# Residual additions of a feed-forward layer by accumulating DMA, and five blocks a layer with all chunks by seven products

## The chip, the cores and the metric

The kernel runs on one core of a Trainium2 chip. The metric is the device time of one execution in microseconds (us); lower is better. The five engines of the core are called PE (TensorE, the matrix engine, with PEld for its weight loads), DVE (VectorE), ACT (ScalarE), POOL (GpSimd) and SP (SyncE, which here only issues DMAs).

## What is computed

One decoder layer over 256 tokens of width 2048: a feed-forward layer, a mixer (attention with selected keys beside a recurrent branch), and a second feed-forward layer, each followed by a layer norm. The change concerns the two feed-forward layers, which are, cut to what matters:

```python
def swiglu(h, w_in, w_out):
    a, b = jnp.split(h @ w_in, 2, axis=-1)        # w_in 2048 x 11264
    return (jax.nn.silu(a) * b) @ w_out           # w_out 5632 x 2048

h = layer_norm(DN_ALPHA * h + 0.5 * swiglu(h, ffn1_w_in[l], ffn1_w_out[l]), ln1_g[l], ln1_b[l])
# ... mixer, layer norm ...
h = layer_norm(DN_ALPHA * h + 0.5 * swiglu(h, ffn2_w_in[l], ffn2_w_out[l]), ln3_g[l], ln3_b[l])
```

All values are float32.

## The kernel before

Every large product is made of three matmuls on two rounded halves: an operand is split into a high part (a rounding copy by ACT) and a low part (the difference, by DVE), and `three` (L597) sums high x high, high x low and low x high into PSUM. For weights this is done piece by piece on the fly: `Weights.load_to` (L153) issues the loads on SP, eight pieces ahead, and `split_to` (L181) makes `wh` on ACT (L209) and `wl` on DVE (L210), four pieces ahead of PE. There are five buffers for each of `wh` and `wl`.

A feed-forward layer goes through 22 blocks of 256 hidden columns (512 columns of `w_in`, a and b together). `blockF` (L623) makes one block's product with `w_in`. The 2048 input rows are four chunks. A **plain** chunk is two pieces of 1024 columns; each piece is 12 matmuls of 512 columns (two row tiles, two token halves, three matmuls). A **fast** chunk uses a seven-product scheme on 2 x 2 sub-blocks (token halves, row tiles against columns a and b): it needs sums of weights, made by DVE (`operand`, L174: the `ws` sum L182 of 1024 columns, the sums L186 and L189 of 512), and sums of the input, made once per layer by `left` (L509). It has four pieces, `p1q3`, `p2`, `q5p7`, `q4p6`, with 12, 6, 12 and 12 matmuls of 256 columns. Its weight tile of 1 MB (`rf`) has two buffers, the plain pieces of 512 KB (`raw`) four, the sums `ws` one. The partial sums of a block lie in two banks `mm` (`c`) and, for the fast chunks, in two banks `bp` (`e`).

The gate of a block (`gate`, L886) joins the partial sums on DVE (L894 to L899), takes silu on ACT and multiplies on DVE (L905). Some pieces later PE transposes the result (L911), and `g` is split like the weights (L724, L725).

The product with `w_out` runs in the same loop. Pieces of it, called fills (`"o"` in a plan), stand between the pieces of later blocks; a fill is 12 matmuls of 512 columns. After two or four fills one 256 x 512 part of the layer's output is complete for one segment of blocks (`SEGS`), and `y_add` (L732) adds half of it to the residual tile `Y` on DVE (L734), once for each token half. The last segment's part is made after the last block, by `out_product`, where `y_add` also takes the statistics of the layer norm.

`block_plan` (L68) writes the order of the pieces in a block and `layer_plans` (L94) those of the 22 blocks. Blocks 0 and 1 are plain; of the rest most have chunks 1 to 3 fast and chunk 0 plain, four fills, and blocks 2 to 5 two or three fast chunks and two fills. From block 9 on the plan of a block is

```
o o c0 p1q3.1 p2.1 q5p7.1 o q4p6.1 p1q3.2 p2.2 c2 q5p7.2 q4p6.2 p1q3.3 o p2.3 q5p7.3 q4p6.3
```

PE, SP and POOL execute in the order in which the program is written; the order on DVE and ACT is a scheduler's, by priority and its own estimate of time. Small tasks (gate, transposes, `left`) are put between the pieces by `Background.step`, one step per piece.

Of the kernel before, what the change touches and what calls it, by code (L numbers as in the profile page):

```python
# [12 lines left out]
OP = mybir.AluOpType  # L13
# [49 lines left out]
PIECE = 1024  # L63
FAST = (1, 2, 3)
FAST_A = (2, 3)


def block_plan(chunks, fills, lead=2, n=4):  # L68
# [6 lines left out]
    plan = [(rest.pop(), 0) for _ in range(min(lead, fills))] + [plain.pop(0)]  # L75
    slow = []
    while plain or rest:
        for which in (rest, plain) if lead == 2 else (plain, rest):
# [200 lines left out]
def tile_layer(ctx, tc, x_fm, x_tm, pos, f1a, f1o, wA, wki, wB, wG, lru, wab, wrb, wo, f2a, f2o,  # L279
# [19 lines left out]
    def T1(s="t"):  # L299
        return pool.tile([P, S], F32, name=name(s), tag="t", bufs=T_BUFS)  # L300

# [72 lines left out]
    W = Weights(nc, pool, pieces, bg.step)  # L374
    W.fast_pool = ctx.enter_context(tc.tile_pool(name="f1", bufs=1))


# [131 lines left out]
    def left(src, forms, k):  # L509


        s = U("sf")
        a = [v.rearrange("p (t c) -> p t c", t=2) for v in src]
        q = s.rearrange("p (f c) -> p f c", f=4)
        V.tensor_tensor(q[:, 0], a[0][:, 1], a[1][:, 1], op=OP.subtract)
        V.tensor_tensor(q[:, 2], a[0][:, 0], a[0][:, 1], op=OP.subtract)
        V.tensor_tensor(q[:, 1], q[:, 0], a[0][:, 0], op=OP.subtract)
        V.tensor_tensor(q[:, 3], a[1][:, 0], q[:, 1], op=OP.add)
        h, l = U("sh", F32R), U("sl", F32R)
        A.activation(h, s, AF.Copy)  # L520
        V.tensor_tensor(l, s, h, op=OP.subtract)
        forms[k] = h, l
# [100 lines left out]
    def blockF(x, forms, plan, fill):  # L623

        c = e = None

        seen = set()
        last = {f: i for i, (f, k) in enumerate(plan)}  # L630
        top = max(last["c"], last.get("p2", 0)), max(last["c"], last.get("q4p6", 0))
        k0 = next(k for f, k in plan if f == "c")
        skip = 0
        if getattr(x, "halves", None):
            c = [MM(), MM()]
            eager(x, c)
            skip = 4
        for i, (form, k) in enumerate(plan):
            if i < skip:
                continue  # L640
            if form == "o":
                fill()
                continue
            if form == "c":
                if not c:
                    c = [MM(), MM()]
                    half = [c[0][:, :S], c[0][:, S:], c[1][:, :S]]
                for k in range(k, k + 2):
                    w = W.unit(512)
                    for t in range(2):  # L650
                        tokens(c[t], x[k], t, w, k == k0, k % 2 == 1 and i == top[t])
                continue
            if not e:
                e = [BP(), BP()]
                p1, p6, p7, q5 = e[0][:, :S], e[0][:, S:], e[1][:, :S], e[1][:, S:]
            start = form not in seen
            seen.add(form)
            stop = i == last[form]
            fs = [forms[2 * k + r] for r in range(2)]

            def xop(r, i, t):
                v = x[4 * k + 2 * r + i]
                return v[:, 0, t * P:(t + 1) * P], v[:, 1, t * P:(t + 1) * P]

            def sop(r, i):
                return tuple(v[:, i * P:(i + 1) * P] for v in fs[r])

            def run(ps, op, start, stop):
                for r in range(2):
                    three(ps, *op(r), W.unit(S), start and r == 0, stop and r == 1)  # L670

            if form == "p1q3":
                run(p1, lambda r: xop(r, 0, 0), start, False)
                run(half[1], lambda r: sop(r, 3), False, False)
            elif form == "p2":
                run(half[0], lambda r: xop(r, 1, 0), False, i == top[0])
            elif form == "q5p7":
                run(q5, lambda r: sop(r, 0), start, False)
                run(p7, lambda r: sop(r, 2), False, stop)
            else:  # L680
                run(half[2], lambda r: xop(r, 1, 1), False, i == top[1])
                run(p6, lambda r: sop(r, 1), False, stop)
        return c, e
# [47 lines left out]

    def y_add(ps, nb, stat, t):  # L732
        y = Y[t][nb]
        V.scalar_tensor_tensor(y, ps[t], 0.5, y, op0=OP.mult, op1=OP.add)  # L734
        if stat:
            V.bn_stats(stats["st"][t][:, nb * 6:nb * 6 + 6], y)  # L736

# [108 lines left out]
    def out_product(x, ln, forms=None, pair=False):  # L846
# [3 lines left out]
        def done(nb, ps, t):  # L850
            y_add(ps, nb, ln, t)
            if ln and nb == 3:
                ln.chain(t)
# [17 lines left out]
        for nb in range(len(ready), 4):  # L871
            if ln and nb == 3:
                ps = blockA(x, lambda ps: end(ps, 0), LAG_LAST if ln.last else LAG_LN,
                            None if ln.last else ln)
                end(ps, 1)
            else:
# [3 lines left out]
                for t in range(2):  # L880
                    done(nb, ps, t)
        if ln and ln.last:
            ln.finish()

    def ffn(x, forms, ln):
        def gate(c, e, g, i, lag):  # L886

# [3 lines left out]
            if e:  # L891
# [5 lines left out]
                for t in range(2):  # L897
                    zt = z[:, t * 512:(t + 1) * 512]
                    V.tensor_tensor(zt, zt, c[t], op=OP.add)  # L899
                A.activation(a, a, AF.Silu)  # L900
# [20 lines left out]
        def fill():  # L921
# [19 lines left out]
        if not ln.last:  # L941
            bg.add("main", later(consts(), W.last.ins))
        out_product(g[-1], ln, pair=True)
# [358 lines left out]
    out_product(mg, ln, mg_forms)  # L1302
    mg = mg_forms = None


# [77 lines left out]
```

## Time and profile before

| | |
|---|---|
| time, median of 3 runs | 2396.58 us (2395.66 to 2397.06) |
| profiled execution, its own time | 2395.88 us |
| its span, first to last instruction | 2394.1 us |
| mean granted clock of PE | 0.998 of full speed |
| PE, DVE, ACT busy | 99%, 92%, 60% of the span |
| DMA | 480.23 MB, mean 201 GB/s |

A page of the profile gives busy time by engine and by group of instructions; a row of a group reads: line, engine, operation, output <- input, shapes, count, then busy us, mean ns of one, and the idle time of the engine just before them with what ended it. A window gives the busy time of each engine in a stretch. A timeline lists instructions with start and duration in us. Instructions of one engine overlap by their start-up, so the pace of an engine is read from the distance between starts.

### The profile page before, as it was taken

How to read it: one execution, taken by the hardware profiler on the slowest of the kernel's cores; microseconds unless marked ns; L12 is line 12 of the kernel's file. 1: busy time of each engine (PE TensorE's matmuls, PEld its weight loads, DVE VectorE, ACT ScalarE, POOL GpSimd, SP SyncE). 2: the span in 40 equal slices, each digit the busy share in tenths (PEclk: the TensorE clock that was granted, in tenths of full speed). 3: DMA queues.
4: the chain of work that ended last, by engine and by line, in shares of the span. 5: the costliest groups of instructions: out<-in, count | busy, mean ns of one | idle time of the engine just before them, and what ended most of it. 6: DMA issues, size and time to landing. Idle time of an engine off the chain costs nothing. (4 is left out here: it accounts for less than half of the span.)

```text
span 2394.1 us, 38065 instructions
## 1 busy us (share of the span) xinstructions
PE 2371.3 (99%) x14674; PEld 2104.5 (88%) x14674; DVE 2209.0 (92%) x3127; ACT 1444.5 (60%) x1934; POOL 54.2 (2%) x118
## 2 busy tenths in 40 slices
PE   9999999999999999999999999999999999999997
PEld 7888889888888888888999998888889888888986
DVE  7999999999999998789788888998999999999997
ACT  7555555555547554665588885545655555555652
POOL 0000000000000000001000001100000000000000
PEclk9999999999999999999999999999999999999999
DMA  8555455555566456547655568755654555556554
GB/s 301 187 206 191 183 211 212 199 197 194 183 186 220 176 185 182 187 142 267 201 183 187 186 192 300 245 194 177 217 204 186 211 198 184 183 201 224 211 191 139
DMA packets 113286, 480.23 MB, mean 201 GB/s; under 512 B 13232, under 2 KB 13232, under 8 KB 93776
## 3 DMA queue, kind: packets, MB, share of 16 engines
q1 hardware_dynamic: 105984, 454.60, 54.1%
q0 software_dynamic: 7120, 23.19, 2.9%
q8 instruction: 115, 1.88, 0.3%
q14 instruction: 67, 0.55, 0.1%
HBM read 467.26 MB, written 10.49 MB: 200 GB/s over the span
## 5 line engine op out<-in xcount | busy, mean ns | idle before, releaser
L209 ACT ACTIVATE wh<-raw 128x1024 fp32r<-128x1024 f32 (+2 forms) x564 | 583.4, 1045 | 390.3 <-PE mm L600 252.0
L210 DVE TENSOR_TENSOR wl<-raw,wh 128x1024 fp32r<-128x1024 f32 (+2 forms) x564 | 669.2, 1197 | 91.6 <-ACT wh L209 89.6
L209 ACT ACTIVATE wh<-rf 128x1024 fp32r<-128x1024 f32 (+1 forms) x453 | 410.6, 916 | 265.3 <-PE mm L600 182.1
L210 DVE TENSOR_TENSOR wl<-rf,wh 128x1024 fp32r<-128x1024 f32 (+1 forms) x453 | 468.5, 1040 | 8.5 <-ACT wh L209 4.8
L598 PE MATMUL mm<-wh,hs 128*128 128x512 f32 (+1 forms) x908 | 329.3, 363 | 0.3 <-DVE z L899 0.3
L600 PE MATMUL mm<-wh,hs 128*128 128x512 f32 (+1 forms) x908 | 323.6, 356 | 1.1 <-DVE hs L786 1.1
L599 PE MATMUL mm<-wl,hs 128*128 128x512 f32 (+1 forms) x908 | 323.2, 356 | 0.2 <-DVE wl L210 0.2
L598 PE MATMUL mm<-wh,g 128*128 128x512 f32 x704 | 280.4, 398 | 0.0
L600 PE MATMUL mm<-wh,g 128*128 128x512 f32 x704 | 278.1, 395 | 0.0
L599 PE MATMUL mm<-wl,g 128*128 128x512 f32 x704 | 277.9, 395 | 0.0
L209 ACT ACTIVATE wh<-ws 128x1024 fp32r<-128x1024 f32 x151 | 160.1, 1061 | 175.2 <-PE mm L600 69.2
L598 PE MATMUL bp<-wh,sh 128*128 128x256 f32 x906 | 254.0, 280 | 0.0
L599 PE MATMUL bp<-wl,sh 128*128 128x256 f32 x906 | 252.9, 279 | 0.7 <-DVE wl L210 0.7
L600 PE MATMUL bp<-wh,sl 128*128 128x256 f32 x906 | 253.2, 279 | 0.0
L210 DVE TENSOR_TENSOR wl<-ws,wh 128x1024 fp32r<-128x1024 f32 x151 | 183.8, 1217 | 18.9 <-ACT wh L209 18.8
L600 PEld LDWEIGHTS mm<-wh,hs 128*128 128x128 f32 x908 | 170.4, 188 | 30.0 <-DVE hs L786 2.5
L598 PEld LDWEIGHTS mm<-wh,hs 128*128 128x128 f32 x908 | 170.6, 188 | 29.2 <-issue 4.4
L599 PEld LDWEIGHTS mm<-wl,hs 128*128 128x128 f32 x908 | 170.7, 188 | 24.7 <-DVE wl L210 0.7
L182 DVE TENSOR_TENSOR ws<-rf 128x1024 f32<-128x1024 f32 x151 | 183.9, 1218 | 4.6 <-DMA rf<-wA 1.4
L1217 PE MATMUL mm<-hs,wh 128*128 128x256 f32 x640 | 179.9, 281 | 0.0
L1216 PE MATMUL mm<-hs,wh 128*128 128x256 f32 x640 | 179.9, 281 | 0.0
L1218 PE MATMUL mm<-hs,wl 128*128 128x256 f32 x640 | 179.9, 281 | 0.0
(293 smaller groups left out, 5093.9 us busy)
## 6 DMA issues: line engine op xcount, KB each, us to landing
rf<-f1a SPq DMA_DIRECT2D x58, 1024.0 KB, 4.9
rf<-f2a SPq DMA_DIRECT2D x58, 1024.0 KB, 5.0
raw<-f1o SPq DMA_DIRECT2D x88, 512.0 KB, 5.8
raw<-f2o SPq DMA_DIRECT2D x88, 512.0 KB, 6.1
raw<-wB SPq DMA_DIRECT2D x80, 512.0 KB, 4.3
raw<-f2a SPq DMA_DIRECT2D x60, 512.0 KB, 4.8
raw<-f1a SPq DMA_DIRECT2D x59, 512.0 KB, 5.5
raw<-wG SPq DMA_DIRECT2D x54, 512.0 KB, 4.3
```

What stands on the lines that cost most here:

```text
L182: v.tensor_tensor(t, b[:, 0:4:3], b[:, 1:2].to_broadcast([P, 2, 2, 256]), op=OP.add)
L209: nc.scalar.activation(hp, src, AF.Copy)
L210: self.last = nc.vector.tensor_tensor(lp, src, hp, op=OP.subtract)
L598: T.matmul(ps, xh, w[0], start=start, stop=False)
L599: T.matmul(ps, xh, w[1], start=False, stop=False)
L600: T.matmul(ps, xl, w[0], start=False, stop=stop)
L1216: T.matmul(ps[:, :S], w[0], x[:, 0], start=first, stop=False)
L1217: T.matmul(ps[:, :S], w[0], x[:, 1], start=False, stop=False)
L1218: T.matmul(ps[:, :S], w[1], x[:, 0], start=False, stop=last)
```

## The change

- The fills' additions to `Y` leave DVE. ACT copies each finished half, times 0.5, from PSUM to a tile `yd`, and a DMA issued by POOL adds it to `Y` in place.
- Blocks 9, 12, 15, 18 and 21 of each layer take all four chunks by seven products; `blockF` no longer needs a plain chunk to open the banks, and starts and stops of the partial sums are worked out per bank.
- The order within blocks changes: every block from 6 on leads with three fills, blocks 3 to 5 all have three fast chunks. A block with four fast chunks is

```
o o o p1q3.0 p2.0 q5p7.0 q4p6.0 p1q3.1 p2.1 q5p7.1 q4p6.1 o p1q3.2 p2.2 q5p7.2 q4p6.2 p1q3.3 p2.3 q5p7.3 q4p6.3
```

- The joining part of the gate is issued at high priority.
- `left` is also made for chunk 0 in feed-forward layers (two calls more a layer). Its result lies in a pool that shares its space with the small tiles `t`, which are not used at that time.

```diff
-FAST = (1, 2, 3)
+FAST = (0, 1, 2, 3)
+BANKS = {"c": (0, 1), "p1q3": (2, 0), "p2": (0,), "q5p7": (3,), "q4p6": (1, 2)}
...
+FOUR = (9, 12, 15, 18, 21)
+
 def layer_plans():
     three = (1, 2, 3)
-    return ([block_plan((), 0)] * 2 + [block_plan((1, 3), 2, 0), block_plan(three, 2)] * 2
-            + [block_plan(three, 4, 3)] * 3 + [block_plan(three, 4)] * 13)
+    plans = [block_plan((), 0)] * 2
+    plans += [block_plan((1, 3), 2, 0)] + [block_plan(three, 2, 2, late=False)] * 3
+    for n in range(6, NBK):
+        plans.append(block_plan(FAST if n in FOUR else three, 4, 3))
+    return plans
...
+    lane, first_home, shared = [None], {}, ExitStack()
+    def share(which):
+        shared.close()
+        p = shared.enter_context(tc.tile_pool(name=name(which), bufs=1))
+        lane[0] = p if which == "t" else None
+        first_home.clear()
+        if which == "s":
+            first_home.update({0: p, 1: p})
...
-        h, l = U("sh", F32R), U("sl", F32R)
+        if k in first_home:
+            h, l = (first_home[0].tile([P, 512], F32R, name=name("s0"), tag="s0", bufs=4) for _ in range(2))
+        else:
+            h, l = U("sh", F32R), U("sl", F32R)
...
                 for t in range(2):
-                    zt = z[:, t * 512:(t + 1) * 512]
-                    V.tensor_tensor(zt, zt, c[t], op=OP.add)
+                    w = 512 if plain or t == 0 else S
+                    zt = z[:, t * 512:t * 512 + w]
+                    V.tensor_tensor(zt, zt, c[t][:, :w], op=OP.add)
...
             if k0 + 2 == len(g[s]):
                 for t in range(2):
-                    y_add(open_ps, nb, False, t)
+                    u = W.fast_pool.tile([P, 512], F32, name=name("yd"), tag="yd", bufs=2)
+                    A.activation(u, open_ps[t], AF.Copy, scale=0.5)
+                    G.dma_start(Y[t][nb], u, accum_op=OP.add)
...
                 c, e = blockF(x, forms, PLANS[n], fill)
-                task = gate(c, e, g[s], 2 * (n - b0), LAG_T[n == NBK - 1])
-                next(task)
+                task = gate(c, e, g[s], 2 * (n - b0), LAG_T[n == NBK - 1], ("c", 0) in PLANS[n])
+                with tc.high_priority():
+                    next(task)
                 bg.add("gate", task)
```

More of the change, by code (lines that the diff above doesn't have):

```diff
@@ L74, in block_plan @@
     rest = ["o"] * fills
-    plan = [(rest.pop(), 0) for _ in range(min(lead, fills))] + [plain.pop(0)]
+    plan = [(rest.pop(), 0) for _ in range(min(lead, fills))] + plain[:1]
+    plain = plain[1:]
     slow = []
     while plain or rest:
-        for which in (rest, plain) if lead == 2 else (plain, rest):
+        for which in (plain, rest) if late else (rest, plain):
             if which:
@@ L627, in blockF @@
         c = e = None
[L629 to L632, printed above, removed]
+        first, last = {}, {}
+        for i, (f, k) in enumerate(plan):
+            for b in BANKS.get(f, ()):
+                first.setdefault(b, i)
+                last[b] = i
         skip = 0
@@ L643, in blockF @@
                 continue
+            if not c:
+                c = [MM(), MM()]
+            start, stop = ([f.get(b) == i for b in range(4)] for f in (first, last))
             if form == "c":
[L645 to L648, printed above, removed]
+                for j in (k, k + 1):
                     w = W.unit(512)
                     for t in range(2):
-                        tokens(c[t], x[k], t, w, k == k0, k % 2 == 1 and i == top[t])
+                        tokens(c[t], x[j], t, w, start[t] and j == k, stop[t] and j > k)
                 continue
@@ L1303, in tile_layer @@
     mg = mg_forms = None
+    share("s")
     ffn(ln.hs, ln.forms, OuterNorm(ln3_g, ln3_b))
```

55 lines of the change are left out of this document (27 added, 28 removed).

## The prediction

> **What bounds the kernel now.** I read the page's engine table first, then the windows of a stretch that is nothing but feed-forward blocks, then the timelines of PE and DVE inside one block, because a share of 99% says that PE is never empty but not how much room the engine behind it has.
>
> ```profile
> PE 2371.3 (99%) x14674; PEld 2104.5 (88%) x14674; DVE 2209.0 (92%) x3127; ACT 1444.5 (60%) x1934; POOL 54.2 (2%) x118
> ...
> 1950.00:2300.00 350.00, 350.00 (x2211) 312.94 (x2210) 339.56 (x406) 206.32 (x242) 1.61 (x3) 1.00 0.55 200
> ```
>
> The second row is the window from 1950 to 2300 us (length; busy PE, PEld, DVE, ACT, POOL; clock; DMA share). PE is busy in all 350.00 us at full clock, DVE in 339.56, or 97.0%; ACT has 41% free. So every matmul cycle taken from these blocks shortens the run, but only while DVE, which makes each weight piece, keeps up. The timelines (start, duration) give both paces:
>
> ```profile
> 2012.90 0.28 PE L598 MATMUL mm<-wh,hs 128*128 128x256 f32 x1
> 2037.87 0.28 PE L598 MATMUL bp<-wh,sh 128*128 128x256 f32 x1
> 2039.27 0.28 PE L598 MATMUL mm<-wh,hs 128*128 128x256 f32 x1
> 2040.78 0.28 PE L599 MATMUL bp<-wl,hs 128*128 128x256 f32 x1
> 2042.07 0.40 PE L598 MATMUL mm<-wh,g 128*128 128x512 f32 x1
> 2044.87 0.28 PE L598 MATMUL mm<-wh,hs 128*128 128x256 f32 x1
> ...
> 2036.65 1.22 DVE L210 TENSOR_TENSOR wl<-rf,wh 128x1024 fp32r<-128x1024 f32 x1
> 2037.79 1.22 DVE L210 TENSOR_TENSOR wl<-raw,wh 128x1024 fp32r<-128x1024 f32 x1
> 2038.93 0.68 DVE L186 TENSOR_TENSOR rf<-ws,rf 128x512 f32<-128x512 f32 x1
> 2039.53 0.68 DVE L210 TENSOR_TENSOR wl<-rf,wh 128x512 fp32r<-128x512 f32 x1
> 2040.13 0.68 DVE L189 TENSOR_TENSOR rf<-rf 128x512 f32<-128x512 f32 x1
> 2040.73 1.22 DVE L210 TENSOR_TENSOR wl<-ws,wh 128x1024 fp32r<-128x1024 f32 x1
> ...
> 2043.17 1.22 DVE L182 TENSOR_TENSOR ws<-rf 128x1024 f32<-128x1024 f32 x1
> 2044.30 1.22 DVE L210 TENSOR_TENSOR wl<-raw,wh 128x1024 fp32r<-128x1024 f32 x1
> ```
>
> Durations overlap, so I go by starts. The fill piece from 2042.07 to 2044.87 is 12 matmuls of 512 columns: 2.80 us, 233.3 ns each. The q5p7 piece from 2037.87 to 2039.27 is 12 matmuls of 256: 1.40 us, 116.7 ns each, exactly half. The rows at 2012.90 and 2044.87 are the same step of two neighbouring blocks: 31.97 us per block. Of that, six plain or fill pieces are 16.80 and three chunks of 42 half-width matmuls 14.70; the other 0.47 are the gate's transposes. DVE takes 1.14 us per 1024-wide operation (2036.65 to 2037.79) and 0.60 per 512-wide one (2038.93 to 2039.53).
>
> The DVE row at 2036.65 writes the low half of the last p1q3 piece of its block; it ends at 2037.87, and PE first uses it at 2040.78. So DVE is 2.9 us ahead there, and this is the smallest such distance I found in that stretch: PE does not wait for DVE, but DVE's whole reserve is about one p1q3 piece and a half.
>
> **The change, PE's part.** A plain chunk is 24 matmuls of 512, 24 x 233.3 = 5.60 us. By seven products it is 42 of 256, 42 x 116.7 = 4.90 us. 0.70 us are saved per chunk. Converted are chunk 0 in the five blocks named in FOUR, and also chunk 2 of block 4, whose plan goes from two fast chunks to three: six a layer, twelve in two layers, 12 x 0.70 = **8.4 us**. The built program agrees on the count: 216 more matmul rows, 12 x 18. Everything from the first layer norm to the second feed-forward layer keeps its instruction order on all engines, so I put no gain or loss there.
>
> On weight loads one rule speaks against splitting matmuls: "TensorE: Matmul & The Clock Gate" of the Trainium skill (Back-to-back issue gap) gives a sustained 131 ns at 512 columns and 81 at 128, so that halving the width saves less than half. An estimate by that page, midway at 256, is 98 ns, a chunk then costs 0.97 us more and the change 12 us. The rows here show 233.3 and 116.7, so the sum stays with the rows.
>
> **DVE's part.** Four things change. (a) The 80 residual additions of the fills, L734, leave DVE:
>
> ```profile
> L734 DVE SCALAR_TENSOR_TENSOR y<-mm,y 128x512 f32<-128x512 f32 x22 | 14.1, 682 | 0.0
> ```
>
> That is the same window, about 11 blocks: 14.1 / 11 = 1.28 us a block. (b) A converted chunk costs DVE the ws sum and three wl of 1024, 4 x 1.14, and one wl and two sums of 512, 3 x 0.60: 6.36 us, against two wl of a plain one, 2.28: +4.1. (c) Chunk 0 needs its left forms, two calls a layer, in blocks 0 and 1, where all is plain and DVE has two 1.14 us operations per 5.6 us of PE: free. (d) In a four-chunk block the second half of the second bank is not added, -0.3 (half of a 512-wide operation).
>
> Per block, DVE now needs 339.56 x 31.97 / 350 = 31.0 us of 31.97. After: a three-chunk block 31.0 - 1.3 = 29.7 against 31.97, 2.3 to spare; a four-chunk block 29.7 + 4.1 = 33.8 against 31.97 - 0.70 = 31.27, **2.5 short**. FOUR has every third block, so three blocks need 93.0 of PE's 95.2 us: DVE can follow on the mean at 97.7%, and the question is whether the reserve lasts through one four-chunk block.
>
> I followed one by its order. Let PE start its first fill at 0. Three fills end at 8.4, then p1q3, p2, q5p7 and the transposes, q4p6 ends at 13.77, chunk 1 at 18.67, the fourth fill at 21.47, chunk 2 at 26.37; in chunk 3 q5p7 is due at 28.47 and q4p6 at 29.87. There are five hi/lo pairs, so chunk 1's p1q3 can be split when the third fill leaves PE at 8.4. The ACT copy before it
>
> ```profile
> L209 ACT ACTIVATE wh<-rf 128x1024 fp32r<-128x1024 f32 x66 | 70.2, 1064 | 26.6 <-PE mm L600 21.5 <-PE bp L600 3.8
> ```
>
> is free to start some 0.2 us later and takes 1.06, so DVE begins at about 9.7. From there its order leaves it no pause: up to the end of chunk 3's q5p7 stand eleven operations of 1.14, eight of 0.60 and two g splits,
>
> ```profile
> L725 DVE TENSOR_TENSOR g<-bp,g 128x256 fp32r<-128x256 f32 x22 | 9.2, 416 | 0.0
> ```
>
> 9.2 / 22 = 0.42 each: 18.2 us in all. Ready at 27.9, due at 28.47: **0.6 us to spare.** q4p6 follows at 29.0, due 29.87; the next block's first fill at 30.2, due 31.27.
>
> Two other covers are as thin. The weight loads: chunk 2's 1 MB tile is loaded into the one that chunk 0's last split frees at about 9.3, and is wanted at 14.7, 5.4 us later:
>
> ```profile
> DMA to landing us min/median/max: 4.8/4.9/7.0
> ```
>
> (the rf loads of the window). The median fits by 0.5 us; a landing of 7.0 takes 1.6 and would use up the cover. And blocks 3 to 5, with two fills, run short of DVE already:
>
> ```profile
> 1765.43 1.21 DVE L210 TENSOR_TENSOR wl<-ws,wh 128x1024 fp32r<-128x1024 f32 x1
> ...
> 1767.92 0.28 PE L599 MATMUL bp<-wl,sh 128*128 128x256 f32 x1
> ```
>
> At the end of block 3 the piece is ready at 1766.64 for 1767.92: 1.3 us ahead. Without L734 it would be 2.6. Such a block is PE 31.97 - 5.60 = 26.37 and DVE 29.7 - 2.28 = 27.4, 1.1 short; today block 4 with two fast chunks lets DVE recover, after the change three short blocks follow each other: 2.6, 1.5, 0.4 ahead. Still no stall; without cover up to 1 us a layer.
>
> **ACT, Pool, DMA.** ACT gains per block two reads of PSUM, 0.6 us each by the nearest row,
>
> ```profile
> L1162 ACT ACTIVATE gt<-mm x10: 577/598/600, 936.9 to 1468.8; 128x512 f32<-128x512 f32 x10
> y<-ys POOLq DMA_DIRECT2D x8, 256.0 KB, 4.3
> 1470.24 4.34 POOL L1169 DMA_DIRECT2D gf<-gd  x8
> ...
> 1471.60 1.23 DVE L182 TENSOR_TENSOR ws<-rf 128x1024 f32<-128x1024 f32 x1
> 1472.74 1.22 DVE L210 TENSOR_TENSOR wl<-raw,wh 128x1024 fp32r<-128x1024 f32 x1
> ```
>
> and 1.06 us for each extra copy. They wait in ACT's queue for the fourth fill to end, at 21.47; behind them is the copy for chunk 3's p1q3, which could not start earlier anyway, because the same fill holds its buffer. 0.2 + 1.2 + 1.06 later, at 23.9, it is there; DVE, by the same count, comes to it at 23.8. That pause takes 0.1 of the 0.6. So I forecast no stall in the four-chunk blocks, with half a microsecond of cover in each. No accumulating DMA is in the trace; by the nearest row a 256 KB transfer issued by Pool lands after 4.3 us, its u tile is wanted again a block later and its Y tile four blocks later. Bounds: 4.3 to 31 us cost nothing, above that ACT would wait. Pool issues one in 0.54 us (eight in 4.34). Whether DVE is held meanwhile: during those eight its 1024-wide operations start 1.14 us apart (1471.60 to 1472.74), as elsewhere, so I take nothing; the other bound is 80 x 0.54 = 43 us of DVE. "SBUF — State Buffer" of the Trainium skill (the rule on the shared port pair) has a DVE operation with two SBUF inputs collide with Pool's reads, not its writes; the rows agree. On Pool's queue ln3's row loads now stand behind the accumulations; only the final normalisation, after the last matmul, wants them.
>
> Small gain: where the plan passes from three leading fills to two, PE waited once a layer for the gate to free its bank. All later blocks lead with three after the change.
>
> ```profile
> L598 PE MATMUL mm<-wh,hs 128*128 128x512 f32 x600 | 241.6, 403 | 0.3 <-DVE z L899 0.3
> ```
>
> 0.3 us, twice. I set it against small waits that thin covers invite.
>
> **Sum.** The profiled execution is 2395.88 us, its span 2394.1; the runs' median 2396.58 is 0.7 above it. Span 2394.1 - 8.4 = 2385.7, and **2388.2 us** against the median. About 0.2%, 4.8 us, is what a measurement of this kernel can tell from no change; faster by that means under 2391.8, slower over 2401.4.
>
> **Rivals.**
> A, the covers fall short by a little. Every number above is a start-to-start time without the spread of 16 queues or of semaphores, and DVE takes its work in a fixed order. A stall of 0.4 to 1.3 us in each of ten four-chunk blocks gives 4 to 13 us back: 2392 to 2401, no difference that can be told. For it: three covers under 0.7 us. Against it: PE had not one stall behind DVE in 350 us at 97.0%. 0.19.
> B, slower: DVE does not bring its reserve back in the three-chunk blocks, because the gate's additions now go first and its pauses stay (the window leaves it 10.4 us in 11 blocks, most of it a wait for ACT).
>
> ```profile
> L210 DVE TENSOR_TENSOR wl<-ws,wh 128x1024 fp32r<-128x1024 f32 x33 | 40.2, 1219 | 6.6 <-ACT wh L209 6.6
> ```
>
> Then each four-chunk block stalls by its whole 2.5 us, or more: 25 - 8.4, 2413. It decides from 1.3 us of stall per four-chunk block. Against it: that wait is for a copy which itself waits for PE to free a buffer, so it goes when DVE is behind. 0.12.
> C, half-width matmuls become bound by their weight loads, 188 ns each instead of 116.7:
>
> ```profile
> L598 PEld LDWEIGHTS mm<-wh,hs 128*128 128x128 f32 x908 | 170.6, 188 | 29.2 <-issue 4.4
> ```
>
> 42 x 188 is 2.3 us above a plain chunk, 12 of them 28 us: 2424. The 1.40 us of q5p7 speak against it. 0.01.
> D, the change does not do what it says: an accumulation lands so late that the last block's sums hold the final additions, which read the same Y tiles. Landing in 4.3 us against some 17 us to the first of them (six fill pieces) speaks against it. All of the 8.4 us would be gone: 2396. 0.02.
> The forecast has 0.66.
>
> **Numbers.** Faster 0.66 + a little of A's edge = 0.67; same 0.20; slower 0.13. The range: from 2386.5 (the two waits, 0.6, and a spread of 1) to 2397, which takes in the forecast and most of A.
>
> **What would show it.** By layer, 144 fewer matmuls of 512 columns and 252 more of 256. Right: PE busy in all of 1950 to 2290, DVE 97 to 98%, blocks of 31.97 and 31.27 us, L734 gone from it. A shows as idle before L599 behind "DVE wl" in blocks 9, 12, 15, 18, 21; a late load as "DMA rf" before L182 or L209. B shows the same idle in neighbouring three-chunk blocks. I am wrong if PE has no stall and the time still does not fall, or if L210's 1.22 us grow while Pool issues.

## The result and the profile after

The changed kernel takes 2393.05 us (median of 19 runs, 2389.72 to 2395.57) against 2396.40 us before (19 runs, 2395.62 to 2397.50). The ratio is 0.9985, 95% interval 0.9978 to 0.9992: faster by 3.35 us, 0.14%, which is less than the 0.2% that the prediction set as the limit of "no change". That is the outcome "same", to which it gave 0.20, not "faster", which had 0.67. The time lies in the range, but 4.9 us of the forecast gain of 8.2 are missing, and the runs spread over 5.9 us where those of before spread over 1.9. The profiled execution is 2391.64 us, its span 2389.9.

First the rows that answer to those shown of before: the page's engine table and the window from 1950 to 2300 us (length; busy PE, PEld, DVE, ACT, POOL; clock; DMA share).

```profile
PE 2364.8 (99%) x14890; PEld 2111.8 (88%) x14890; DVE 2213.9 (93%) x3127; ACT 1501.9 (63%) x2042; POOL 124.4 (5%) x198
...
1950.00:2300.00 350.00, 350.00 (x2279) 316.87 (x2278) 343.00 (x406) 222.66 (x271) 19.24 (x22) 1.00 0.65 215
```

PE is still busy in all 350 us. DVE went from 339.56 to 343.00, 98.0%; ACT gained 16 us, Pool 18. Counted over the whole trace at 2.80 us for twelve matmuls of 512 columns, the matmuls' own columns fell from 2327.3 to 2318.9 us, by 8.40: the forecast saving is there to the second decimal. From the start of the first matmul to that of the last, the time beyond those columns went from 48.4 to 53.6 us. (The stretches before the first and after the last matmul are together 1.0 us shorter; nothing in the forecast stands for that.) So 5 us more were lost between matmuls, and the group table says where most of it is (two rows of after, then the same two of before):

```profile
L623 PE MATMUL mm<-wh,g 128*128 128x512 f32 x704 | 278.9, 396 | 3.1 <-DVE z L921 3.1
...
L624 PE MATMUL bp<-wl,sh 128*128 128x256 f32 x918 | 256.4, 279 | 1.3 <-DVE wl L218 1.3
...
L598 PE MATMUL mm<-wh,g 128*128 128x512 f32 x704 | 280.4, 398 | 0.0
...
L599 PE MATMUL bp<-wl,sh 128*128 128x256 f32 x906 | 252.9, 279 | 0.7 <-DVE wl L210 0.7
```

The second row, pauses behind a weight piece, is 0.6 us above its counterpart of before. The first is new: one pause of 3.1 us behind the gate's additions. It stands in the timeline of PE (start, duration, and in brackets the idle time and its releaser) right after block 21 of the second layer, at the start of the output product:

```profile
2335.97 0.40 PE L625 MATMUL mm<-wh,g 128*128 128x512 f32 x1
2339.43 0.47 PE L623 MATMUL mm<-wh,g 128*128 128x512 f32 x1 [3.07 <-DVE z L921]
...
2340.24 0.63 PE L623 MATMUL mm<-wh,g 128*128 128x512 f32 x1
2340.66 0.63 PE L624 MATMUL mm<-wl,g 128*128 128x512 f32 x1
...
2343.62 0.40 PE L625 MATMUL mm<-wh,g 128*128 128x512 f32 x1
2343.85 0.39 PE L623 MATMUL mm<-wh,g 128*128 128x512 f32 x1
```

From 2335.97 to 2339.43 are 3.46 us, 3.23 more than a matmul's 0.23. Behind it matmuls start 0.42 us apart instead of 0.23 for 3.4 us: the twelve steps from 2339.43 to 2343.85 take 4.42 us, where 12 x 0.233 = 2.80 are due, 1.6 more. Pause and slow stretch make 4.8 us. The windows of that stretch show both, and beside them DVE and ACT with nothing to do. The last row is one window of the kernel before:

```profile
2320.00:2325.00 5.00, 5.00 (x46) 5.00 (x45) 4.92 (x7) 3.05 (x5) 4.71 (x9) 1.00 1.00 203
2325.00:2330.00 5.00, 5.00 (x36) 4.59 (x35) 5.00 (x6) 3.97 (x5) 0.54 (x1) 1.00 0.93 244
2330.00:2335.00 5.00, 5.00 (x23) 4.02 (x22) 2.06 (x3) 0.00 (x0) 0.00 (x0) 1.00 0.96 355
2335.00:2340.00 5.00, 1.93 (x9) 1.26 (x8) 2.54 (x4) 3.18 (x4) 0.00 (x0) 1.00 0.53 197
2340.00:2345.00 5.00, 5.00 (x16) 3.92 (x15) 3.63 (x4) 2.42 (x3) 0.00 (x0) 0.66 0.79 265
...
2330.00:2335.00 5.00, 5.00 (x33) 4.45 (x33) 4.46 (x5) 3.08 (x3) 0.00 (x0) 1.00 0.28 73
```

ACT is at 0.00 and DVE at 2.06 of 5 us one window before PE stops, while the DMA engines are full (0.96; 0.28 in the same window of before). So this is a load that came late, not a DVE that is too slow. Who filled the DMA engines is in the timeline of Pool:

```profile
2319.16 1.75 POOL L955 DMA_DIRECT2D y<-yd  x2 [25.37 <-ACT yd L954]
2320.24 1.24 POOL L593 DMA_DIRECT2D gr<-ln_g  x1
2320.80 1.25 POOL L593 DMA_DIRECT2D br<-ln_b  x1
...
2323.72 0.99 POOL L593 DMA_DIRECT2D gr<-ln_g  x1
2325.25 0.54 POOL L593 DMA_DIRECT2D br<-ln_b  x1 [0.55 <-PE mm L625]
```

After the last two accumulations come all eight row loads of ln3, 256 KB each, in 5 us. In the kernel before, Pool's queue was empty, and each went out when its buffer came free: at 2191.94, 2203.87, 2205.28 and from 2306.11 to 2311.76. Now they stand behind the accumulations, which wait for ACT's copies of the last fill. The weight loads that SP issues next, by their line in the window from 2327 to 2333:

```profile
L176 SPq DMA_DIRECT2D raw<-f2o x4: 328/328/328, 2327.3 to 2331.1; - x4
...
  ACT wh L217: 7.9, 3
...
DMA to landing us min/median/max: 8.9/9.0/9.2
```

They land after 9.0 us. Four such loads of the kernel before, in its window from 2334 to 2340:

```profile
DMA to landing us min/median/max: 3.7/4.8/5.2
```

The queue table of the trace from 2325 to 2329, and then from 2329 to 2334, has as packets, MB and share of the 16 engines

```profile
q0 software_dynamic: 268, 0.90, 86.9%
...
q0 software_dynamic: 283, 0.90, 57.9%
q1 hardware_dynamic: 209, 0.79, 41.4%
```

No packet of SP's queue (q1) was moved in the first of the two, though loads were issued at 2327.3 and 2328.5. The first one moves at 2330.7, 3.4 us after the issue; in e1 and e10 below, where the engines are free by then, it moves 0.9 to 1.0 us after it. From 2330.7 on the two queues share. "DMA: Bandwidth & Descriptors" of the Trainium skill (Queues, rings and completion order) says that each engine goes round between the queues it has work for, a packet at a time; the sharing after 2330.7 agrees with that. The wait of 3.4 us before it, with Pool's queue alone on full engines, is not explained by it, and its cause stays open.

What is late next, in the timelines of ACT and of DVE:

```profile
2336.38 1.06 ACT L217 ACTIVATE wh<-raw 128x1024 fp32r<-128x1024 f32 x1 [7.41 <-DMA raw<-f2o]
...
2330.95 0.42 DVE L916 TENSOR_TENSOR z<-z,bp 128x256 f32<-128x256 f32 x1
2331.40 0.69 DVE L917 TENSOR_TENSOR z<-bp,z 128x512 f32<-128x512 f32 x1
2337.46 1.23 DVE L218 TENSOR_TENSOR wl<-raw,wh 128x1024 fp32r<-128x1024 f32 x1 [5.37 <-ACT wh L217]
2338.61 1.01 DVE L921 TENSOR_TENSOR z<-z,mm 128x512 f32<-128x512 f32 x2
```

The load lands, ACT copies it at 2336.38, DVE splits it at 2337.46. Between the gate's subtraction (L917) and its additions (L921) DVE's order has the split of just this piece. The additions could have run at 2332, when the subtraction is done; they sit behind a piece that PE doesn't need yet, and PE waits for them, because they free the c bank in which the next product begins. This last link is read from the timelines; no run changed that order alone.

### The profile page after: what moved, and what is told of

Read it like the earlier page. It is cut to its first block, busy times and chain, and to the rows that moved or that the text cites. A ratio compares the mean times of both kernels' runs of the same rounds, so it can differ in the third digit from the quotient of the medians.

```text
span 2389.9 us, 38777 instructions
## 1 busy us (share of the span) xinstructions
PE 2364.8 (99%) x14890; PEld 2111.8 (88%) x14890; DVE 2213.9 (93%) x3127; ACT 1501.9 (63%) x2042; POOL 124.4 (5%) x198
## 5 line engine op out<-in xcount | busy, mean ns | idle before, releaser
L217 ACT ACTIVATE wh<-raw 128x1024 fp32r<-128x1024 f32 (+2 forms) x540 | 552.2, 1044 | 295.1 <-PE mm L625 166.0
L218 DVE TENSOR_TENSOR wl<-raw,wh 128x1024 fp32r<-128x1024 f32 (+2 forms) x540 | 637.7, 1198 | 100.3 <-ACT wh L217 98.7
L217 ACT ACTIVATE wh<-rf 128x1024 fp32r<-128x1024 f32 (+1 forms) x489 | 440.0, 915 | 314.8 <-PE mm L625 157.9
L218 DVE TENSOR_TENSOR wl<-rf,wh 128x1024 fp32r<-128x1024 f32 (+1 forms) x489 | 506.5, 1042 | 13.1 <-ACT wh L217 7.4
L623 PE MATMUL mm<-wh,hs 128*128 128x512 f32 (+1 forms) x884 | 317.1, 359 | 0.0
L625 PE MATMUL mm<-wh,hs 128*128 128x512 f32 (+1 forms) x884 | 311.1, 352 | 1.1 <-DVE hs L807 1.1
L624 PE MATMUL mm<-wl,hs 128*128 128x512 f32 (+1 forms) x884 | 310.8, 352 | 0.2 <-DVE wl L218 0.2
L217 ACT ACTIVATE wh<-ws 128x1024 fp32r<-128x1024 f32 x163 | 172.9, 1061 | 141.8 <-PE mm L625 81.5
L190 DVE TENSOR_TENSOR ws<-rf 128x1024 f32<-128x1024 f32 x163 | 198.7, 1219 | 5.8 <-DMA rf<-f1a 1.2
L218 DVE TENSOR_TENSOR wl<-ws,wh 128x1024 fp32r<-128x1024 f32 x163 | 198.7, 1219 | 2.8 <-ACT wh L217 2.6
L625 PEld LDWEIGHTS mm<-wh,hs 128*128 128x128 f32 x884 | 165.8, 188 | 27.5 <-DVE hs L807 2.5
L623 PEld LDWEIGHTS mm<-wh,hs 128*128 128x128 f32 x884 | 166.1, 188 | 24.3 <-issue 1.3
```

The lines of the kernel that those rows point to most:

```text
L190: v.tensor_tensor(t, b[:, 0:4:3], b[:, 1:2].to_broadcast([P, 2, 2, 256]), op=OP.add)
L217: nc.scalar.activation(hp, src, AF.Copy)
L218: self.last = nc.vector.tensor_tensor(lp, src, hp, op=OP.subtract)
L623: T.matmul(ps, xh, w[0], start=start, stop=False)
L624: T.matmul(ps, xh, w[1], start=False, stop=False)
L625: T.matmul(ps, xl, w[0], start=False, stop=stop)
```

## Experiments

Theory T: the whole loss is the burst of row loads at the tail, because they now stand behind the accumulations in Pool's queue. Theory C: the thin covers of the four-chunk blocks (DVE's reserve of half a microsecond) set it; this is rival A of the prediction, not its C. Each time below is a median of 5 to 11 runs, beside runs of the kernel before.

**e1_rows_late**: the eight loads go to SP's queue, behind the last weight load.

```diff
-    def row(v, nb, s):
+    def row(v, nb, s, eng=G):
...
+            self.rows = [(row(self.g, nb, "gr", nc.sync), row(self.b, nb, "br", nc.sync)) for nb in range(4)]
...
                     for t in range(2):
                         done(nb, ready[nb], t)
+            ln.prepare()
...
-        ln.prepare()
```

> The changed kernel, with ln3's eight row loads (gr, br) moved off POOL's queue to SP's, behind the last weight load of the layer. Theory T (tail): the changed kernel loses its missing 5 us at one place, after block 21 of the second layer, where these eight loads and two accumulations make a fill's weights land after 9.0 us; then PE has no stall near 2339 us, its clock stays full there, and the time is 2387 to 2389, with runs within 1.5 us of each other. Theory C (cover): the loss lies in the four-chunk blocks, where DVE is only 0.2 to 0.3 us ahead; then the time stays at 2391 to 2393 with the same spread.

Measured: 2387.99 us (2387.86 to 2388.73), ratio 0.9966, interval 0.9953 to 0.9978. That is 5.1 us under the changed kernel and 0.2 under the forecast of 2388.2. DVE's timeline at the place in question:

```profile
2332.53 0.69 DVE L918 TENSOR_TENSOR z<-bp,z 128x512 f32<-128x512 f32 x1
2333.13 1.22 DVE L218 TENSOR_TENSOR wl<-raw,wh 128x1024 fp32r<-128x1024 f32 x1
2334.26 1.02 DVE L922 TENSOR_TENSOR z<-z,mm 128x512 f32<-128x512 f32 x2
```

The order is the same, the split comes 0.6 us behind the subtraction instead of 6.1, and PE has no pause there. The spread of the runs is down to 0.9 us. The weight loads issued from 2328.4 to 2332.2 land after 4.6 us in the median. T holds for the place; the accumulations themselves, all 80 still there, cost nothing that shows.

**e2_no_four** and **e4_shift** change the covers and leave the burst.

```diff
-FOUR = (9, 12, 15, 18, 21)
+FOUR = ()                       # e2_no_four
+FOUR = (8, 11, 14, 17, 20)      # e4_shift
```

> The changed kernel with FOUR empty: no block takes all four chunks by seven products; additions by DMA, order of pieces and row loads stay. PE's work is then 7.0 us more than in the changed kernel and 1.4 less than before. Both theories expect DVE to be 2 us or more ahead in the blocks from 6 on. T: the burst of row loads is still there, but DVE is about 2.5 us further ahead at the end of block 21 and covers most of it: 2394 to 2396. C: 2394.5, with no spread. If accumulating DMAs cost time by themselves: above 2397.

> The changed kernel with the four-chunk blocks one earlier, 8, 11, 14, 17, 20, so that the last block is a three-chunk one; same PE work, row loads as in the changed kernel. T: the burst of loads remains but meets a DVE that is 2 to 3 us further ahead, so the stall after block 21 shrinks from 3.2 to under 1 and the clock stays full: 2388 to 2390. C: the same five tight blocks a layer, so no change: 2391 to 2393.

Measured: e2 2400.37 us (2398.17 to 2402.61; ratio 1.0016, 1.0007 to 1.0024), e4 2391.86 (2390.33 to 2393.60; 0.9981, 0.9972 to 0.9990). Both miss what T forecast, and e4's time lies in C's band, e2's where "accumulating DMAs cost time by themselves" had put it. The traces decide: PE's pause behind the same additions is 3.4 us in e2, which has no four-chunk block at all, and 2.6 in e4, where block 21 is a three-chunk block.

```profile
L623 PE MATMUL mm<-wh,g 128*128 128x512 f32 x704 | 279.2, 397 | 3.4 <-DVE z L921 3.4
```

(e2, group table.) I had expected that a DVE with more in hand would hide part of the burst. The two runs don't test that alone: their accumulations and row loads also go out later, beside the weight loads and not ahead of them, and these land after 12.6 us in e2 and 12.0 in e4 (medians of four), not 9.0. As for the accumulations by themselves, e1 has all 80 of them, and e1 plus the 7.0 us of columns is 2395.0; e2's other 5.4 us are about the price of the burst. This speaks against C more strongly than e1: with the four-chunk blocks gone, the pause is still there. It also prices the four-chunk blocks: without them the columns of PE are 7.0 us longer, and the run is 7.3 longer.

**e10_half**: four of the eight loads stay in the burst, four go late.

```diff
-            self.rows = [(row(self.g, nb, "gr"), row(self.b, nb, "br")) for nb in range(4)]
+            self.b_rows = [row(self.b, nb, "br") for nb in range(4)]
+
+        def prepare_late(self):
+            self.rows = [(row(self.g, nb, "gr", nc.sync), self.b_rows[nb]) for nb in range(4)]
...
+            if ln.last:
+                ln.prepare_late()
```

> The kernel after the change with half of the burst: the four row loads of the bias stay on Pool's queue behind the accumulations, the four of the gain go to SP's queue behind the last weight load, as all eight do in e1_rows_late. 1.0 MB instead of 2.1 MB beside the last raw loads. At some 400 GB/s in which the DMA engines were busy, a row load of 256 KB takes 0.65 us of all of them; four fewer are 2.6 us. If the delay goes with the bytes queued: the raw load lands 2.6 us earlier, at some 6.4 instead of 9.0, the pause of 3.2 us is down to 0.6 or less, and the clock stays up: 2388 to 2389. If what counts is Pool's queue as such (one transfer from it is enough to put the raw load last), the pause stays: 2391 to 2393.

Measured: 2387.37 us (2386.72 to 2388.43), ratio 0.9962 (0.9950 to 0.9975). The weight loads of the window 2327 to 2333:

```profile
DMA to landing us min/median/max: 3.6/4.9/5.0
```

Half the bytes take away the whole delay, not half of it: the four row loads are through by 2328.5, and at 2328.1 the first of these weight loads is issued. So Pool's queue as such does no harm; what counts is whether its transfers are still in flight when the load is issued.

**e5_rows_early**: the row loads are put ahead of block 19.

```diff
+                if n == 19:
+                    ln.prepare()
...
-        ln.prepare()
```

> The kernel after the change, with the eight row loads of the last layer norm (256 KB each, written into the shared U buffers) put on Pool's queue ahead of block 19 of each layer instead of after block 21; they stay Pool's, and the last ten or so accumulations stand behind them. Theory T (the loss at the tail is the burst: eight row loads behind two accumulations in 6 us, just when the last weight load is in flight): the burst is no longer beside the last weight load, so the pause of 3.2 us and the slow clock behind it go: 2387.5 to 2390. A cost may come instead, where a row load waits in Pool's queue for its U buffer and the accumulations behind it wait with it: then ACT's next copy waits for its u tile and the fourth fill's bank is freed late; one such wait would be a pause of PE in blocks 19 to 21, and the time up to 2395. Theory C (thin cover in the four-chunk blocks sets the loss): nothing changes, 2393.

Measured: 2388.74 us (2388.02 to 2389.22), ratio 0.9970 (0.9958 to 0.9981). Six of the eight go out between 2227.1 and 2230.6, as close as at the tail, and the weight loads issued from 2222 to 2236 by the line of the raw and rf loads are as late:

```profile
DMA to landing us min/median/max: 6.5/10.4/11.8
```

PE has no pause there. Much the same burst is free inside the blocks and costs 4.8 us at the tail. The time lies where T had put it.

**e6_before_burst**, **e9_before_held**, **e12_before_held2**: the burst in the kernel before, without one accumulation.

```diff
-        ln.prepare()
+        with tc.issue_after(W.last.ins):      # e6
+            ln.prepare()
...
+        if ln.last:
+            G.dma_start(mark[0:1, :64], Y[1][3][0:1, :64])        # e9
+            G.dma_start(mark[0:1, :64], g[-1][-4][0:1, 1, :64])   # e12
         ln.prepare()
```

> The kernel before the change, without one accumulating DMA and with its old additions and plans; only the eight row loads of the last layer norm are held back until the last weight load of the second feed-forward layer has been issued, so that Pool issues them in one burst there. Theory T in its strict form (the row loads alone are enough): the last raw load or the copies behind it come late, PE pauses 2 to 4 us at the tail, the granted clock falls for some matmuls: 2399.5 to 2402. Rival (the burst hurts only together with accumulations, or only a DVE that is as thin as after the change): no pause, 2396.4. The last weight load is issued ahead of the rows here, not behind them, so a middle result (1 to 2 us) would say that only transfers queued ahead of the load count.

> The kernel before the change, with its own additions on DVE, its own plans and no accumulating DMA. Added is one small DMA on Pool's queue, 64 floats of a Y tile after the last fill's addition to a scratch tensor, ahead of the last layer norm's eight row loads: it changes nothing of the result and moves no bulk, but the row loads stand behind it and can only be issued after about 2320 us, as in the changed kernel. This is the test that e6_before_burst was to be (there the row loads went out at the times of before, so it compared nothing). Theory T, that the place of the row loads in Pool's queue is the cause, and no accumulation is needed: eight row loads within some 6 us, the raw load beside them lands after 8 us or more, PE pauses 2 to 4 us near 2340 and the clock falls behind it: 2398.5 to 2401. Rival, that the burst hurts only where DVE's cover is as thin as after the change: a pause of under 1 us, 2396 to 2396.5.

> The kernel before the change, as in e9_before_held, but the small DMA ahead of the eight row loads reads a g tile of block 20 that DVE finishes at 2319.6 us, so that the row loads go out from about 2320 to 2325 as in the changed kernel, 14 us earlier than in e9_before_held. No accumulating DMA, no thinner DVE. If the burst alone costs what it costs after the change (a raw load issued beside it lands after 9 us, PE pauses some 3 us near 2340, the clock falls behind it): 2400 to 2402. If the two accumulations ahead of it or the thinner DVE are a part of that price: 1 to 2 us, 2397.5 to 2399. If the raw loads of before are issued at other moments than after the change, so that none stands behind the burst: 2396.4.

e6 (2395.79 us beside 2395.63, ratio 1.0000, 0.9991 to 1.0008) made no burst: its row loads went out from 2191.27 to 2311.04 like those of before. It compares nothing. e9 gave 2397.93 us beside 2396.43 (1.0006, 0.9997 to 1.0015), its burst from 2334.28 to 2338.84. e12 gave 2396.14 beside 2396.29 (0.9999, 0.9990 to 1.0008), its burst from 2320.30 to 2326.17. In both the weight loads beside the burst are late. First e9, the loads issued from 2335.1 to 2338.8; then e12, the one issued at 2326.7; then the kernel before, that same load, issued at 2326.9:

```profile
DMA to landing us min/median/max: 6.6/11.3/12.1
```

```profile
DMA to landing us min/median/max: 10.1/10.1/10.1
```

```profile
DMA to landing us min/median/max: 3.5/3.5/3.5
```

So the burst alone, with no accumulation near it, delays the loads. What PE loses differs; e9's time lies between what T and its rival had forecast, e12's is that of its last alternative, but not for the reason given there, since a load did stand behind the burst. In e9 it pauses twice:

```profile
2353.70 0.50 PE L598 MATMUL mm<-wh,g 128*128 128x512 f32 x1 [0.34 <-ACT g L724]
...
2355.03 0.51 PE L600 MATMUL mm<-wh,g 128*128 128x512 f32 x1 [0.59 <-DVE g L725]
```

That is 1.25 us in starts, and the median of the runs rises by 1.5: again not the late piece itself, but a small step (g's split, L724 and L725) that stands behind it in the order of ACT and DVE. In e12 PE loses nothing. Its ACT:

```profile
2330.05 1.06 ACT L209 ACTIVATE wh<-raw 128x1024 fp32r<-128x1024 f32 x1 [0.34 <-PE mm L600]
2332.85 2.02 ACT L209 ACTIVATE wh<-raw 128x1024 fp32r<-128x1024 f32 x2 [1.73 <-PE mm L600]
2336.94 1.06 ACT L209 ACTIVATE wh<-raw 128x1024 fp32r<-128x1024 f32 x1 [2.08 <-DMA raw<-f2o]
```

Three loaded pieces were still to be copied when the late load was issued, at 2326.7, so ACT waits for it 2.08 us, not 7.41, and the gate's additions come at 2341.82 instead of 2340.13, still before PE wants their bank. After the change ACT had copied all the loaded pieces by 2328.7. T in its strict form, the same price without any accumulation, is not shown. The kernel before is some 7 us further back in its work at the same time (its last matmul starts at 2381.2, that of e1 at 2373.9), so e12's burst meets it that much too early and e9's, 14 us later, some 7 too late. A burst at just the same step was not tried. Nor does either run have the two accumulations ahead of the row loads. In e1, where those two are alone in flight, the DMA engines are 0.96 to 1.09 full from 2322 to 2324 at 160 to 188 GB/s, so they are probably a part of the burst's price.

**e3_dve_add**: the fills' additions back on DVE, the four-chunk blocks kept.

```diff
-                    u = W.fast_pool.tile([P, 512], F32, name=name("yd"), tag="yd", bufs=2)
-                    A.activation(u, open_ps[t], AF.Copy, scale=0.5)
-                    G.dma_start(Y[t][nb], u, accum_op=OP.add)
+                    y = Y[t][nb]
+                    V.scalar_tensor_tensor(y, open_ps[t], 0.5, y, op0=OP.mult, op1=OP.add)
```

> The changed kernel with the fills' additions back on DVE (no copy on ACT, no accumulating DMA), five four-chunk blocks a layer as in the changed kernel. By DVE's account three blocks then need 96.8 us of DVE against 95.2 of PE: 1.6 us of stall for each four-chunk block, 16 in all, and some in blocks 3 to 5: 2400 to 2406, slower than before the change. If DVE had room left after all, 2388.

Measured: 2417.58 us (2416.99 to 2418.04), ratio 1.0088 (1.0074 to 1.0101). The window from 1950 to 2300:

```profile
1950.00:2300.00 350.00, 343.14 (x2235) 309.87 (x2234) 347.42 (x417) 208.50 (x245) 1.61 (x3) 1.00 0.56 201
```

DVE at 99.3% holds PE for 6.9 us of 350. The direction was expected, the size was not: PE's time beyond its columns is 79.3 us, 29.4 more than in e1. Of that, each of the ten four-chunk blocks pauses by 1.9 to 2.1 us, 20.4 in all where 16 were expected, and blocks 3 to 5 of both layers add 7.1. I had counted that three-chunk blocks pay in advance for the four-chunk ones; with five hi/lo pairs DVE can be ahead only so far, and what it has over beyond that is lost. e2 shows the cap: by the prediction's account every three-chunk block leaves DVE 2.3 us, all blocks from 6 on are such blocks there, and yet its lead at the last q5p7 piece of a block stays at 2.9 to 3.5 us from 1917 to 2333. e3 speaks for T as well: with no accumulation in Pool's queue the row loads go out between 2204 and 2332 as before, and PE does not pause after block 21, though DVE has less to spare here than after the change.

**e7_alternate** (on e1): seven four-chunk blocks a layer.

```diff
-FOUR = (9, 12, 15, 18, 21)
+FOUR = (9, 11, 13, 15, 17, 19, 21)
```

> The kernel of e1_rows_late with seven four-chunk blocks a layer instead of five: 9, 11, 13, 15, 17, 19, 21. PE's own sum falls by 2 x 2 x 0.70 = 2.8 us more. A pair of blocks needs 29.7 + 33.8 = 63.5 us of DVE for 63.24 of PE, and only one three-chunk block stands between two four-chunk ones, in which DVE can win back at most what its buffers hold. If a surplus is carried in full: 2385.2. If DVE's lead after a single three-chunk block is some 0.7 us lower than after two, each of the 14 four-chunk blocks stalls 0.4 to 1.2 us: 2391 to 2402. A result under 2387 would say that the limit of five a layer is not DVE.

Measured: 2391.83 us (2391.03 to 2392.60), ratio 0.9983 (0.9974 to 0.9992): 3.8 us slower than e1, although PE has 2.8 us less to do. The pauses behind a weight piece, e7 and then e1:

```profile
L624 PE MATMUL bp<-wl,sh 128*128 128x256 f32 x918 | 257.7, 281 | 4.2 <-DVE wl L218 4.2
```

```profile
L624 PE MATMUL bp<-wl,sh 128*128 128x256 f32 x918 | 256.4, 279 | 1.3 <-DVE wl L218 1.3
```

Ten four-chunk blocks now pause by 0.43 to 0.47 us each (start to start). One three-chunk block between two of them doesn't refill DVE's reserve; two do: at the last q5p7 piece ahead of a four-chunk block DVE's lead is 2.1 us in e7 and 3.3 in e1.

**e8_no_priority** (on e1): the gate's first part without its priority.

```diff
-                with tc.high_priority():
-                    next(task)
+                next(task)
```

> The kernel of e1_rows_late without the priority that the change gives to the first part of the gate (the additions of the sums into z): they take their place in DVE's order as before the change. If the priority matters little: 2388, as e1. If the additions then come behind the next block's weight pieces, PE waits for the c or e banks at the second lead fill or at the first q5p7 of each block, 0.3 to 1 us in some of the 32 blocks with three chunks or more: 2392 to 2410. If the priority costs more than it brings (the weight pieces come late because of it), 2386 to 2387.

Measured: 2388.25 us (2387.25 to 2388.83), ratio 0.9966 (0.9954 to 0.9979), no difference from e1.

**e11_late_shift** (on e1): the four-chunk blocks one place earlier, as in e4.

> The kernel of e1_rows_late with the five four-chunk blocks one place earlier (8, 11, 14, 17, 20), so that block 21 is a three-chunk block and DVE goes into the output product with more ahead. The only pause that e1_rows_late showed after a block 21 is 1.0 us in the first layer. If it is DVE's thin lead: that pause goes, 2387.0 to 2387.5. If it is the plan's change from fills to the output product: 2388. A four-chunk block only two places behind blocks 3 to 5 could stall instead, since those leave DVE 0.1 to 0.2 us ahead: up to 1 us in each layer, 2389 to 2390.

Measured: 2387.27 us (2387.14 to 2388.40), ratio 0.9962 (0.9948 to 0.9976). The pause of 1.0 us after block 21 of the first layer is 0.5. But it is 0.5 in e8 and 0.6 in e10 too, where block 21 is as in e1, so it varies by itself and the run does not tell its cause. Against e1 the difference of 0.7 us is too small to claim. e1, e8, e10 and e11 beat both kernels, with ratios of 0.9962 to 0.9966 to the kernel before.

## Why the prediction was right or wrong, step by step

**PE's part: right.** 8.40 us fewer in the columns; e1, which has everything but the burst, runs at 2387.99 for a forecast of 2388.2. That it comes within 0.2 is in part luck: in its profiled execution the time beyond the columns is 1.5 us above that of before, and the stretches before the first and after the last matmul are 1.0 us shorter.

**DVE's part: right, with thinner covers.** The forecast was 97.7% on the mean and half a microsecond in hand in a four-chunk block, with no stall. The timelines of DVE and PE at the end of block 12 of the second layer:

```profile
2037.94 1.22 DVE L218 TENSOR_TENSOR wl<-ws,wh 128x1024 fp32r<-128x1024 f32 x1
...
2039.41 0.28 PE L624 MATMUL bp<-wl,sh 128*128 128x256 f32 x1
```

The q5p7 piece is ready at 2039.16 and used at 2039.41: 0.25 us ahead, and 0.25 to 0.30 in eight other four-chunk blocks, where the ledger gave 0.5. (Its "2.5 short" leaves out the 0.3 us of point (d), which the 93.0 us for three blocks have in them.) In block 18 of this layer nothing was left: PE takes the piece as it comes, 0.1 us late. The page counts no wait in any of them. The wait that B rested on went as its own counter-argument said:

```profile
L218 DVE TENSOR_TENSOR wl<-ws,wh 128x1024 fp32r<-128x1024 f32 x36 | 43.9, 1219 | 0.0
```

In the same window of before this group waited 6.6 us for ACT; now 0.0, since DVE is the one behind. The mean of 1219 ns is that of before to the nanosecond, while Pool issues: DVE is not held.

**Blocks 3 to 5: a little short.** Forecast were 2.6, 1.5 and 0.4 us ahead and no stall. In the second layer the piece came late once:

```profile
1815.75 1.22 DVE L218 TENSOR_TENSOR wl<-ws,wh 128x1024 fp32r<-128x1024 f32 x1
...
1817.03 0.38 PE L624 MATMUL bp<-wl,sh 128*128 128x256 f32 x1 [0.56 <-DVE wl L218]
```

0.7 us in starts, inside the "up to 1 us a layer" that the text kept as the other end. The small gain of 0.3 us behind the gate's bank came (that group now waits 0.0).

**Accumulations: dearer than the row taken for them, and free all the same.** Pool's group over the whole run, and the landing by its line:

```profile
L955 POOL DMA_DIRECT2D y<-yd x80 | 70.1, 982 | 1209.8 <-ACT yd L954 1159.6 <-DVE rf L194 24.9 <-DVE wl L218 24.6
...
DMA to landing us min/median/max: 3.3/6.7/10.0
```

An issue takes 0.98 us in the mean, not 0.54, and lands after 6.7, not 4.3. The landing is inside the bounds of 4.3 to 31 us that cost nothing, and DVE shows no trace of the longer issue. The rf loads of the window took 5.6 us in the median instead of 4.9, past the 5.4 that the text had given them; still, no read of an rf waited in that window, so this cover was counted too tight.

**The step that failed** is the last one of the part on ACT, Pool and DMA: "On Pool's queue ln3's row loads now stand behind the accumulations; only the final normalisation, after the last matmul, wants them." Both halves are true, and the price put on it was nothing. I asked who waits for the moved transfers, and not whom they meet on the way. Held back until 2319 they go out together, the DMA engines stay full to 2335, and the weight loads issued from 2327 to 2331 land after 9.0 us instead of 4.8. PE then waits 3.23 us for the gate's additions, which stand behind the late piece in DVE's order, and loses 1.6 more to the lower clock. The forecast lacked this term: 4.8 us in the profiled run, 5.1 between the medians of the changed kernel and e1. It probably also makes the spread of the runs, which is 0.9 us without the burst; only one of them was traced.

**The rivals.** A's band (2392 to 2401) holds the measured time, but for another reason: its place, the ten four-chunk blocks, shows no stall. The range had been stretched to 2397 for A, so that the time lies in it is luck. What B feared, a reserve that is not brought back, did not occur here. It does once DVE has more to do: about 2.0 us per four-chunk block in e3, with the additions back on DVE, and 0.45 in e7. B's own reason is not what acts there: the gate's priority makes no difference (e8). C and D did not occur: q5p7 still starts every 116.7 ns, and the accumulations land within 10.0 us.

## What to carry to other kernels

When a change puts new work on a queue, look at what already stood in that queue and when it used to go out: transfers that were spread by their buffers can come out in one burst, and the price is paid by a load on another queue. In a fixed order, ask of each late load what small step stands behind it on ACT and DVE; here it was the gate's additions, not the piece itself, that PE waited for. A reserve is capped by its buffers: a surplus beyond them (five pairs here) doesn't pay for a later block.

## What the runs showed of the hardware that I had not expected

The clock falls after a short pause. After 3.07 us without matmuls (the bracket in the timeline above) the granted clock of the next window is 0.66, and for 3.4 us matmuls of 512 columns start 0.42 us apart instead of 0.23; in e2 a pause of 3.4 us is followed by 0.68. After e4's pause of 2.59 us it stays at 1.00 (window 2340 to 2345), and after e9's two short ones, 0.34 and 0.59, too. If one length of pause decides, it lies between 2.59 and 3.07 us in these runs. The drop comes late: the slow steps begin at 2340.24, 0.8 us after PE has started again. "TensorE: Matmul & The Clock Gate" of the Trainium skill (Part 1) gives an idle window of about 3.4 us to half clock, and as long to come back. The way back agrees; the pause that was enough here is a little shorter.

Four row loads of 256 KB ahead of a weight load cost it nothing (4.9 us to landing in the median), eight cost it some 4 us (9.0): between the two lies the moment at which the earlier bytes are through.

An accumulating DMA holds the engines longer than its bytes say. By the queue tables of the two pages, Pool's queue went from 2.9% to 8.1% of the engines' span for 80 accumulations of 256 KB: an estimate of 1.55 us of all sixteen engines each. At the more than 400 GB/s at which weight loads move on full engines (1.00 and 410 GB/s from 2319 to 2320 after the change) the same bytes take 0.65.
